# Sharing one buffer pool between activation pairs and every second weight pair in a down projection

## The chip, the cores and the metric

The kernel runs on one core of one Trainium2 chip. The metric is the device time of one execution in microseconds (us); the time of a kernel is the median of its runs. Beside the times there is one profiled execution of the kernel before, with a record of each instruction on the engines TensorE (PE), VectorE (DVE), ScalarE (ACT), GpSimd (POOL) and on the DMA-issuing queue of SyncE (SP).

## The reference, cut to what matters

The reference is one layer of a decoder trunk over 1024 tokens of 1024 channels, all in float32: a token mixer, then a feed-forward block. The change lies in the last step of the feed-forward block, the down projection:

```python
def _conv_ffn(h, ffn_up, ffn_conv_w, ffn_conv_b, ffn_down):
    hid = h @ ffn_up.astype(h.dtype)
    hid = _causal_dwconv(hid, ffn_conv_w, ffn_conv_b)
    gate, up = hid[..., :D_FF], hid[..., D_FF:]
    return (jax.nn.gelu(gate, approximate=True) * up) @ ffn_down.astype(h.dtype)
...
x = x + _rms_norm(f, norm_post_ffn[i])
```

The gated activations are 1024 x 2816 and `ffn_down` is 2816 x 1024. Behind the product come a norm over the 1024 channels and the addition of the residual.

## The kernel before, in words

**Pairs.** Each float32 operand of a matmul is split into a high part, rounded by a cast on ACT, and a low part, the rest, from a subtraction on DVE or POOL (`split`, L153 to L156). A product of two operands is three matmuls: high by high, high by low and low by high. Activations are split on ACT and DVE, streamed weights on ACT and POOL. All tiles here are 128 x 512.

**Seven products.** The down projection (`ffn_down`, L949) cuts the activations into two token halves and two halves of the 2816 rows (A11, A12, A21, A22), the weights likewise (B11 to B22), and takes seven products in place of eight, in a scheme of Strassen's kind. This text calls them P1 to P7, in the order of the code: P1 A11 by B11, P2 a difference of activations by a sum of weights, P3 A12 by B21, P4, P5 and P6 combinations, P7 the last activation combination by B22. The combined weights were summed earlier and lie in memory as `sums`. Each product goes over 11 pieces j (HT = 11). A piece is one activation pair and one weight pair, and 12 matmuls on them: 3 for each of four 128-token tiles t, each into its own PSUM bank. Four banks X take P1, P3, P5 and P7, four banks Y take P2, P4 and P6.

**Work between the products.** After piece j's activation is split, a function `then(j)` runs: in P4 `after4` (A22 gets A21 added), in P5 `after5` (A11 is replaced by A22 less A11) and in P6 `after6` (A12 is replaced by A12 less A11); each is one DVE operation on two SBUF tiles (L959). They depend on one another and on the tiles, not on the matmuls of their product. When a product is done, its four banks are taken away by `after(t)`. Behind P6 that is `second`, which finishes the second token half, behind P7 `last`; both end in `ffn_out` (L932), which loads the residual x, takes the norm's factor (DVE, then POOL) and writes the output.

**Buffers.** Activation pairs of all products share `h1p`, a pool of 16 tiles, so 8 pairs; before the down projection the same 16 tiles hold the normed activations of the up projection. Streamed weights land in `wr` (3 tiles); their pairs use `wh` and `wl`, 2 tiles each. `f2p` has 6 tiles, for s3 in P2, the junk output of squares, the raw held weights and the residual x.

**Held weights.** The last HELD = 7 weight pairs of P7 are loaded and split early, by `hold`, called from `after5` (at every third j) and `after6` (at every second j). Their pairs lie in `hp`, a pool of 16 tiles which holds A21 and the first five tiles of A22 until these have been used: the k-th held pair needs tiles 2k and 2k+1 free. Their low parts come from DVE (`split(hi, lo, raw, not held)`). P7 runs its first 4 pieces over all four banks, and then the 7 held pieces bank by bank, 21 matmuls for each, so that a bank can be taken away while the next one is worked on.

**Order.** Each engine runs its own queue in order. A planner fixes these queues when the kernel is built, from priorities and its own estimates. Splits, `then(j)` and the weights' loads are in `high_priority` blocks and go ahead of the rest as soon as their buffers are free; buffers of a pool are handed out in the order of the program.

Lines that matter: L156 `split`'s two operations, L163 the weights' load, L129 the matmuls, L959 the DVE operations in `tt`, L993 the squares in `norm`, L939 and L945 residual load and output, L944 the last DVE operation.

Of the kernel before, what the change touches and what calls it, by code (L numbers as in the profile page):

```python
# [12 lines left out]
F32 = mybir.dt.float32  # L13
F32R = mybir.dt.float32r
# [7 lines left out]
P = 128  # L22
# [16 lines left out]
HT = FT // 2  # L39
# [2 lines left out]
LN_EPS = 1e-5  # L42
GN_EPS = 64e-5

HELD = 7
DECAY = math.exp(-0.5)


# [46 lines left out]
class Trunk:  # L95
# [35 lines left out]
    def after(self, i, first):  # L131

        self.tc.add_manual_dep(
            i.ins, first.ins.name,
            mybir.DependencyInfo(mybir.DependencyClass.NoSync, mybir.DependencyReason.DATA),
            reason="the bank's first matmul clears it")
# [18 lines left out]
        eng = self.nc.gpsimd if pool else self.nc.vector  # L155
        return self.nc.scalar.copy(hi, src), eng.tensor_tensor(lo, src, hi.bitcast(F32), ALU.subtract)  # L156

    def weight(self, src, shape, home=None, held=False):

        with self.tc.high_priority():  # L160
            raw = (self.f2p.tile(shape, F32, tag="f2", name=self.nm("wr")) if held else
                   self.wp.tile(shape, F32, tag="wr", bufs=3, name=self.nm("wr")))
            self.nc.sync.dma_start(raw, src)  # L163
            if held:
                hi, lo = (self.hp.tile(shape, F32R, tag="h", name=self.nm("w")) for _ in range(2))
            elif home:
                hi, lo = (home[0].tile(shape, F32R, tag=t, bufs=BUFS[t], name=self.nm("wm")) for t in home[1:])
            else:
                hi, lo = (self.wp.tile(shape, F32R, tag=t, bufs=2, name=self.nm(t)) for t in ("wh", "wl"))
            self.low = self.split(hi, lo, raw, not held)[1]  # L170
        return hi, lo


# [773 lines left out]
    def ffn_down(self, acts):  # L947
        nc = self.nc
        first = self.tc.high_priority  # L949
        A11, A12, A21, A22 = acts[0][:HT], acts[0][HT:], acts[1][:HT], acts[1][HT:]  # L950
        B = lambda r, c: lambda j: self.a["ffn_down"][c, r * HT + j]
        T = lambda n: lambda j: self.sums[n - 1, j]
        X = [self.bank() for _ in range(4)]
        Y = [self.bank(("pb", "pn")[t // 2]) for t in range(4)]
        halves = lambda: [row[:, c * 512:(c + 1) * 512] for row in (self.row("nrow", 4) for _ in range(2)) for c in range(2)]
        four = lambda: [self.tp.tile([P, 512], F32, tag="tp", name=self.nm("c")) for _ in range(4)]

        def tt(out, a, b, op=ALU.add):
            nc.vector.tensor_tensor(out, a, b, op)  # L959
            return out  # L960

        def s3(j):
            return tt(self.f2p.tile([P, HALF], F32, tag="f2", name=self.nm("s3")), A11[j], A21[j], ALU.subtract)

        def product(banks, src, wt, start, after, then=lambda j: None, held=(), soon=True):
            ops, n = [], HT - len(held)
            for j in range(HT):
                with first():
                    hi, lo = self.pair("a", self.h1p)
                    self.split(hi, lo, src(j))  # L970
                    then(j)
                wh, wl = self.weight(wt(j), [P, 512]) if j < n else held[j - n]
                op = (hi, wh), (hi, wl), (lo, wh)
                if j >= n:
                    ops.append(op)
                else:
                    for t in range(4):
                        mms(banks[t], t, op, start and j == 0, j == HT - 1)

            ins = []  # L980
            for t in range(4):
                for i, op in enumerate(ops):
                    ins += mms(banks[t], t, op, False, i == len(held) - 1)
                with first() if soon else ExitStack():
                    after(t)
            self.chain(ins)

        def mms(ps, t, op, start, stop):
            return [self.mm(ps, a[:, t * P:(t + 1) * P], w, start=start and i == 0, stop=stop and i == 2, skip=True)
                    for i, (a, w) in enumerate(op)]  # L990

        def norm(h, t, c, f, src, junk):
            nc.scalar.activation(junk, src, AF.Square, accum_out=self.fss[:, 4 * h + t, c:c + 1])  # L993
            tt(f, src, self.post_ffn[:, c * 512:(c + 1) * 512], ALU.mult)

        s1, s7 = halves(), halves()
        product(X, lambda j: A11[j], B(0, 0), True, lambda t: nc.scalar.copy(s1[t], X[t]))
        product(Y, s3, T(3), True, lambda t: nc.scalar.copy(s7[t], Y[t]))
        c11 = four()
        product(X, lambda j: A12[j], B(1, 0), False, lambda t: norm(  # L1000
            0, t, 0, c11[t], X[t], self.f2p.tile([P, 512], F32, tag="f2", name=self.nm("junk"))))
        c21 = four()
        late = []

        def hold(j, every=2):

            if j % every == 1 and len(late) < HELD:
                late.append(self.weight(B(1, 1)(HT - HELD + len(late)), [P, 512], held=True))


        def after4(j):
            tt(A22[j], A21[j], A22[j])

        def after5(j):
            hold(j, 3)
            tt(A11[j], A22[j], A11[j], ALU.subtract)

        def after6(j):
            hold(j)
            tt(A12[j], A12[j], A11[j], ALU.subtract)  # L1020

        product(Y, lambda j: A22[j], T(4), False, lambda t: tt(c21[t], s1[t], Y[t]), after4)
        product(X, lambda j: A22[j], T(1), True, lambda t: tt(s7[t], s7[t], X[t]), after5)

        def second(t):
            tt(c21[t], c21[t], Y[t])
            tt(s1[t], s1[t], Y[t])
            norm(1, t, 0, c21[t], c21[t], Y[t])
            tt(s7[t], s7[t], s1[t])
            norm(1, t, 1, s7[t], s7[t], Y[t])  # L1030
            self.ffn_out(4 + t, (c21[t], s7[t]))

        def last(t):
            tt(s1[t], s1[t], X[t])
            norm(0, t, 1, s1[t], s1[t], X[t])
            self.ffn_out(t, (c11[t], s1[t]))

        product(Y, lambda j: A11[j], T(2), True, second, after6, soon=False)
        product(X, lambda j: A12[j], B(1, 1), False, last, held=late)
# [258 lines left out]
```

## Time and profile before

| | |
|---|---|
| median of 3 runs | 1340.19 us (1337.7 to 1342.9) |
| the profiled execution | 1338.02 us, of which the span is 1336.2 us |
| mean granted TensorE clock in it | 0.982 |
| PE busy | 1266.3 us of the span, 95% |
| DVE busy | 860.7 us, 64% |
| ACT busy | 679.6 us, 51% |
| POOL busy | 618.8 us, 46% |

Times in the trace count from the start of the span. The down projection runs from about 1089 us to the end. PE is the busiest engine by far, so what matters is where it is not busy, and why. "Idle before" with a releaser in a row of the trace is the time for which the engine had nothing running, and who ended it.

### The profile page before, as it was taken

The page shows a single profiled execution, that of the slowest core. Times are in us where ns is not written, and L with a number is a line of the kernel's source. Part 1 is how long each engine was busy: PE and PEld are TensorE (multiplying, and loading weights), DVE is VectorE, ACT ScalarE, POOL GpSimd, SP SyncE. Part 2 cuts the span into 40 slices and gives each one's busy share as a digit, 9 for nine tenths or more (in the row PEclk, how much of TensorE's full clock was granted, in tenths as well). Part 3 has the DMA queues.
Part 4 walks back from the last instruction along what each step waited for, and adds up shares of the span by engine and source line. Part 5 has one row for each costly group of instructions (what it writes and reads, how often), then busy time and mean ns, then how long its engine had stood idle before and what let it go on. Part 6 is the DMA issues. An engine that isn't in the chain of part 4 may idle for free. (4 is left out here: it accounts for less than half of the span.)

```text
span 1336.2 us, 22956 instructions
## 1 busy us (share of the span) xinstructions
PE 1266.3 (95%) x8580; PEld 1019.7 (76%) x8580; DVE 860.7 (64%) x1450; ACT 679.6 (51%) x1354; POOL 618.8 (46%) x522
## 2 busy tenths in 40 slices
PE   6999989999899989999999999999999989996996
PEld 5767767777678767787798788888888878875885
DVE  5377998997799989885521463455555365295347
ACT  6563654657755765656543564333333344443451
POOL 4343423354333322444462467667676454445441
PEclk9999979999999999999999999999999999997998
DMA  6322211222123441222355655665654323343325
GB/s 213 79 77 62 72 40 49 52 69 56 50 66 104 149 144 50 64 72 79 103 162 172 234 197 179 199 191 178 197 177 139 95 79 95 95 122 123 95 80 204
DMA packets 85647, 155.79 MB, mean 117 GB/s; under 512 B 9280, under 2 KB 15808, under 8 KB 85536
## 3 DMA queue, kind: packets, MB, share of 16 engines
q1 hardware_dynamic: 85536, 154.33, 38.1%
q8 instruction: 67, 1.10, 0.4%
q14 instruction: 44, 0.36, 0.1%
HBM read 129.13 MB, written 25.17 MB: 115 GB/s over the span
## 5 line engine op out<-in xcount | busy, mean ns | idle before, releaser
L156 POOL TENSOR_TENSOR wl<-wr,wh 128x512 fp32r<-128x512 f32 x350 | 474.9, 1358 | 548.9 <-ACT wh L156 522.2
L129 PE MATMUL pb<-f,wh 128*128 128x512 f32 x1408 | 442.3, 395 | 3.2 <-ACT pb L771 1.8
L156 ACT CAST wh<-wr 128x512 fp32r<-128x512 f32 x350 | 215.1, 615 | 326.5 <-PE pb L129 167.4
L129 PEld LDWEIGHTS pb<-f,wh 128*128 128x128 f32 x1408 | 263.7, 188 | 61.9 <-ACT pb L771 2.0
L129 PE MATMUL pb<-f,wl 128*128 128x512 f32 x704 | 280.1, 398 | 2.0 <-POOL wl L156 2.0
L129 PE MATMUL pb<-h,wh 128*128 128x512 f32 (+3 forms) x720 | 229.8, 399 | 2.5 <-ACT wh L156 1.9
L877 DVE SCALAR_TENSOR_TENSOR acc<-pb,params,acc 128x511 f32<-128x511 f32 (+1 forms) x128 | 95.5, 746 | 183.8 <-ACT acc L872 123.9
L399 DVE SCALAR_TENSOR_TENSOR pc<-c,params,pc 128x512 f32<-128x512 f32 x232 | 174.2, 751 | 4.6 <-ACT pc L396 0.5
L129 PEld LDWEIGHTS pb<-f,wl 128*128 128x128 f32 x704 | 132.6, 188 | 35.7 <-POOL wl L156 5.4
L129 PEld LDWEIGHTS pb<-h,wh 128*128 128x128 f32 (+2 forms) x720 | 132.3, 189 | 34.4 <-ACT wh L156 4.3
L129 PE MATMUL pb<-h,wl 128*128 128x512 f32 (+3 forms) x360 | 146.7, 408 | 3.0 <-POOL wl L156 2.8
L129 PE MATMUL pb<-wh,a 128*128 128x512 f32 x428 | 141.9, 400 | 3.4 <-ACT wh L156 3.4
L129 PEld LDWEIGHTS pb<-wh,a 128*128 128x128 f32 x428 | 81.4, 191 | 23.8 <-ACT wh L156 4.3
L129 PE MATMUL pb<-wl,a 128*128 128x512 f32 x214 | 86.7, 405 | 11.3 <-POOL wl L156 11.3
L129 PEld LDWEIGHTS pb<-h,wl 128*128 128x128 f32 (+2 forms) x360 | 68.1, 189 | 22.3 <-POOL wl L156 5.8
L156 DVE TENSOR_TENSOR a<-act,a 128x512 fp32r<-128x512 f32 x50 | 37.3, 746 | 66.1 <-ACT a L156 66.1
L156 ACT CAST a<-act 128x512 fp32r<-128x512 f32 x50 | 31.0, 621 | 71.7 <-PE pn L129 47.5
L129 PEld LDWEIGHTS pb<-wl,a 128*128 128x128 f32 x214 | 41.1, 192 | 23.1 <-POOL wl L156 13.3
L877 DVE SCALAR_TENSOR_TENSOR pt<-pb,params,pt 128x511 f32<-128x511 f32 (+1 forms) x48 | 35.8, 746 | 33.7 <-ACT ecarry L874 33.1
L917 POOL TENSOR_TENSOR b<-b,b 128x512 f32<-128x512 f32 x44 | 57.0, 1295 | 0.9
L872 ACT ACTIVATE acc<-pb,params 128x512 f32<-128x512 f32 x64 | 49.5, 774 | 1.8 <-PE pb L129 1.8
L129 PE MATMUL pn<-wh,a 128*128 128x512 f32 x132 | 47.8, 403 | 0.0
(297 smaller groups left out, 1928.3 us busy)
## 6 DMA issues: line engine op xcount, KB each, us to landing
wr<-ffn_up SPq DMA_DIRECT2D x176, 256.0 KB, 2.7
wr<-w_in SPq DMA_DIRECT2D x80, 256.0 KB, 2.6
b<-ffn_down SPq DMA_DIRECT2D x44, 256.0 KB, 4.0
sums<-b SPq DMA_DIRECT2D x44, 256.0 KB, 2.4
wr<-sums SPq DMA_DIRECT2D x44, 256.0 KB, 2.6
wr<-ffn_down SPq DMA_DIRECT2D x33, 256.0 KB, 2.6
wr<-w_out SPq DMA_DIRECT2D x32, 256.0 KB, 2.7
mixd<-t SPq DMA_DIRECT2D x16, 256.0 KB, 3.2
```

The lines of the kernel that those rows point to most:

```text
L129: return self.nc.tensor.matmul(out, lhsT, rhs, start=start, stop=stop, skip_group_check=skip)
L156: return self.nc.scalar.copy(hi, src), eng.tensor_tensor(lo, src, hi.bitcast(F32), ALU.subtract)
L399: nc.vector.scalar_tensor_tensor(out, c[:, j:j + HALF], w(j), acc, ALU.mult, ALU.add)
L872: nc.scalar.activation(acc, ps, AF.Identity, scale=w(2), bias=self.par("fb", ch))
L877: nc.vector.scalar_tensor_tensor(acc[:, o:], ps[:, :HALF - o], w(j), acc[:, o:], ALU.mult, ALU.add)
L917: sub = lambda o, x, y, op=ALU.subtract: nc.gpsimd.tensor_tensor(o, x, y, op)
```

## The change

Weight pairs of odd pieces (j = 1, 3, 5, ...) of all seven products no longer take `wh`/`wl` but a pair from `h1p`, the activations' 16 tiles; even pieces keep `wh`/`wl` to themselves. HELD goes from 7 to 5, so P7 streams 6 pieces and holds 5. The low part of a held weight is now made on POOL, like that of any other weight. The raw tile of an odd piece still comes from `wr`; only that of a held weight comes from `f2p`.

```diff
-HELD = 7
+HELD = 5
...
-    def weight(self, src, shape, home=None, held=False):
+    def weight(self, src, shape, home=None, held=None):
 
         with self.tc.high_priority():
-            raw = (self.f2p.tile(shape, F32, tag="f2", name=self.nm("wr")) if held else
+            raw = (self.f2p.tile(shape, F32, tag="f2", name=self.nm("wr")) if held is self.hp else
                    self.wp.tile(shape, F32, tag="wr", bufs=3, name=self.nm("wr")))
             self.nc.sync.dma_start(raw, src)
             if held:
-                hi, lo = (self.hp.tile(shape, F32R, tag="h", name=self.nm("w")) for _ in range(2))
+                hi, lo = self.pair("w", held)
             elif home:
...
-            self.low = self.split(hi, lo, raw, not held)[1]
+            self.low = self.split(hi, lo, raw, True)[1]
...
-                wh, wl = self.weight(wt(j), [P, 512]) if j < n else held[j - n]
+                wh, wl = self.weight(wt(j), [P, 512], held=self.h1p if j % 2 else None) if j < n else held[j - n]
...
-                late.append(self.weight(B(1, 1)(HT - HELD + len(late)), [P, 512], held=True))
+                late.append(self.weight(B(1, 1)(HT - HELD + len(late)), [P, 512], held=self.hp))
```

`pair` takes two 128 x 512 tiles from the pool it is given.

## The prediction

> **What bounds the kernel now.** I read the page first: PE is busy for 95% of the span, so only its gaps count. The table by stage, one row for a product, shows where they are.
>
> ```profile
> span 1336.2 us, 22956 instructions
> ```
>
> ```profile
> core 0: us, PE busy (x) PEld busy (x) DVE busy (x) ACT busy (x) POOL busy (x), PEclk, DMA share, GB/s
> ...
> 1186.80:1232.50 45.70, 34.44 (x132) 25.93 (x131) 32.08 (x47) 17.29 (x35) 22.44 (x11) 0.85 0.43 138
> 1232.50:1263.30 30.80, 30.80 (x133) 24.80 (x133) 11.15 (x17) 12.56 (x22) 14.21 (x12) 1.00 0.35 94
> ...
> 1294.40:1325.60 31.20, 31.18 (x134) 24.79 (x132) 27.45 (x52) 11.16 (x29) 7.89 (x9) 1.00 0.42 136
> ```
>
> P5, the middle row, runs at PE's pace: 133 matmuls in 30.80 us; so does P7 below it. P4, the first row, takes 45.70 us for 132. At P5's pace these are 30.6 us, so P4 loses 15.1 us. The timeline of PE shows how, and a second, smaller loss at the start of P1.
>
> ```profile
> 1089.33 1.09 PE L129 MATMUL pb<-wh,a 128*128 128x512 f32 x4
> 1093.92 0.80 PE L129 MATMUL pb<-wl,a 128*128 128x512 f32 x1 [3.50 <-POOL wl L156]
> ...
> 1097.07 1.32 PE L129 MATMUL pb<-wh,a 128*128 128x512 f32 x5
> ```
>
> ```profile
> 1205.62 0.74 PE L129 MATMUL pb<-wh,a 128*128 128x512 f32 x2 [3.04 <-ACT wh L156]
> ...
> 1214.68 0.79 PE L129 MATMUL pb<-wl,a 128*128 128x512 f32 x1 [7.49 <-POOL wl L156]
> ...
> 1219.95 0.40 PE L129 MATMUL pb<-wl,a 128*128 128x512 f32 x1
> ```
>
> Both times PE waits for the low part of a weight. In P4, at j = 5, it first waits 3.04 us for the high part, then 7.49 us for the low one, and after so long an idle time the next 12 matmuls, from 1214.68 to 1219.95, take 5.27 us in place of 2.8 (the granted clock is 0.85 in P4's row): 2.5 us more. At the start of P1 it is 3.50 us idle, and 7 matmuls from 1093.92 to 1097.07 that take 3.15 us in place of 1.6: 5.0 us in all. Next, why POOL and ACT were late.
>
> ```profile
> 1168.48 1.29 POOL L156 TENSOR_TENSOR wl<-wr,wh 128x512 fp32r<-128x512 f32 x1 [1.51 <-ACT wh L156]
> ...
> 1205.64 10.21 POOL L156 TENSOR_TENSOR wl<-wr,wh 128x512 fp32r<-128x512 f32 x2 [5.93 <-ACT wh L156]
> ```
>
> ```profile
> 1203.91 0.62 ACT L156 CAST w<-wr 128x512 fp32r<-128x512 f32 x1 [5.98 <-DVE act L959]
> ```
>
> ```profile
> 1168.64 1.68 DVE L959 TENSOR_TENSOR act<-act,act 128x512 f32<-128x512 f32 x1
> ...
> 1206.20 0.68 DVE L156 TENSOR_TENSOR a<-act,a 128x512 fp32r<-128x512 f32 x1
> 1206.80 1.28 DVE L959 TENSOR_TENSOR act<-act,act 128x512 f32<-128x512 f32 x2
> 1208.01 0.69 DVE L156 TENSOR_TENSOR a<-act,a 128x512 fp32r<-128x512 f32 x1
> ...
> 1212.22 1.29 DVE L959 TENSOR_TENSOR act<-act,act 128x512 f32<-128x512 f32 x2
> ```
>
> A split on POOL costs 1.29 us. A DVE operation on two SBUF tiles comes every 0.60 us when they follow one another (1206.20, 1206.80, and 1208.01 after two more). The two engines exclude each other: the DVE operation at 1168.64 takes 1.68 us because POOL had begun at 1168.48 and ended at 1169.77. The other way round it is worse: from 1206.20 to 1213.5 DVE never pauses, and the POOL split begun at 1205.64 comes through only behind that run (two splits take 10.21 us where they cost 2.6). ACT was late for the same reason: its queue stood 5.98 us in front of a held weight's cast, which waited for `after4` on DVE to free a tile of `hp`, with P4's own cast behind it.
>
> The Trainium skill ("SBUF — State Buffer", section "Who interferes with whom") has the exclusion: a DVE instruction with two SBUF inputs contends with a GpSimd instruction that reads SBUF, and whichever issues first holds the pair for its whole instruction. The 1.68 us row agrees. By that text POOL's turn would come after one DVE instruction; here the row at 1205.64 shows it waiting through a dozen. If POOL did get its turn each time, the sum below would end at its lowest loss, 5.2 us in P4.
>
> How full is that common resource? The groups of DVE and POOL from 1167.26 to 1214.64:
>
> ```profile
> L959 DVE TENSOR_TENSOR act<-act,act 128x512 f32<-128x512 f32 x17 | 14.6, 871 | 0.1
> L156 DVE TENSOR_TENSOR a<-act,a 128x512 fp32r<-128x512 f32 x13 | 10.0, 768 | 2.1 <-ACT a L156 2.1
> L959 DVE TENSOR_TENSOR row<-act,row 128x512 f32<-128x512 f32 x8 | 9.5, 1186 | 0.2
> L959 DVE TENSOR_TENSOR act<-act,row 128x512 f32<-128x512 f32 x8 | 7.4, 920 | 0.0
> L156 DVE TENSOR_TENSOR w<-wr,w 128x512 fp32r<-128x512 f32 x6 | 4.5, 766 | 0.0
> L959 DVE TENSOR_TENSOR c<-pb,post_ffn 128x512 f32<-128x512 f32 x4 | 2.6, 677 | 0.0
> ```
>
> ```profile
> L156 POOL TENSOR_TENSOR wl<-wr,wh 128x512 fp32r<-128x512 f32 x13 | 26.1, 2013 | 22.8 <-ACT wh L156 22.8
> ```
>
> 52 DVE operations with two SBUF inputs (17 + 13 + 8 + 8 + 6) at 0.60 us are 31.2 us; 12 whole POOL splits (the 13th only begins there) at 1.29 us are 15.5 us. Together 46.7 us of 47.4: the pair is full for the whole stretch. Its load is the 33 operations of `after4` to `after6`, which run here all at once though P6 and P7 need most of them much later. So the bound in P4 is this common port, and the weights, only two ahead, pay first.
>
> **The change, part by part.**
>
> *More lead for weights, less for activations.* A weight pair is needed 2.80 us after the one before it:
>
> ```profile
> 1239.81 1.29 POOL L156 TENSOR_TENSOR wl<-wr,wh 128x512 fp32r<-128x512 f32 x1 [1.51 <-ACT wh L156]
> 1242.61 1.29 POOL L156 TENSOR_TENSOR wl<-wr,wh 128x512 fp32r<-128x512 f32 x1 [1.51 <-ACT wh L156]
> ```
>
> Now the pair for j + 2 is free when j is done: 2.80 us of lead. Afterwards even pieces wait for j - 4, so 8.4 us, or 5.6 us where pieces 10 and 0 meet; odd pieces share 8 pairs in which two pieces take three, a lead of 11.2 us. Activations fall from 19.6 us (8 pairs ahead) to 11.2 or 14. This by itself adds no instruction; DMA loads keep their three raw tiles in front.
>
> *The crowded stretch moves.* P4's first activation pair was the ninth from P3's first and came free after piece 3:
>
> ```profile
> 1167.26 0.62 ACT L156 CAST a<-act 128x512 fp32r<-128x512 f32 x1 [1.66 <-PE pb L129]
> ```
>
> In the new order (a0 a1 w1 a2 a3 w3 a4 a5 w5 ...) the ninth pair is w5, two pieces later: 1167.3 + 5.6 = 1172.9. From there I add what must be through before P4's last piece can run, at the same prices. DVE: 11 splits and 33 operations of `after4` to `after6`, 44 x 0.60 = 26.4 us. POOL: the last weight of P3 and the 11 of P4, 12 x 1.29 = 15.5 us.
>
> *Held weights.* Their low parts leave DVE (6 in the stretch, 3.6 us, counted out above) and go to POOL: four of the five come ahead of P4's last weight, 4 x 1.29 = 5.2 us. For the shared port this is a loss of 1.6 us, and in POOL's queue P4's and P5's weights stand behind them.
>
> Sum: 26.4 + 15.5 + 5.2 = 47.1 us, so the last piece's operands are there at 1220.0. Unhindered, PE starts piece 10 at 1186.8 + 28.0 = 1214.8. P4 then loses 5.2 us where the turns fall well. It loses 7.6 if the four `c` operations (2.4 us, one input from PSUM) don't fit beside POOL, and up to 10.1 if the idle time comes in one piece and brings the 2.5 us of slow matmuls again. I take 7, near the middle: the old stretch had 46.7 of 47.4 us filled without the `c` operations, so most of these do fit beside POOL, but DVE's unbroken runs remain. Gain in P4: 15.1 - 7 = 8.1 us. After P4 the port has room (P5's row: DVE 11.15 and POOL 14.21 of 30.80), so nothing new is late there.
>
> *Start of P1.* The unbroken DVE run there is these operations:
>
> ```profile
> L156 DVE TENSOR_TENSOR a<-row,a 128x512 fp32r<-128x512 f32 x7 | 4.5, 684 | 0.0
> L959 DVE TENSOR_TENSOR s<-row,act 128x512 f32<-128x512 f32 x4 | 2.5, 686 | 0.0
> ```
>
> Two of the first eight pairs now go to w1 and w3, so up to two splits (1.2 us) leave the run; w0 keeps its two buffers, and w1's split may stand before it in POOL's queue (1.29 us). Bounds: 1.3 us lost to 5.0 us gained; I take 1 us gained, two splits fewer being the certain part.
>
> *The end.* With five held pairs a bank's last group is 15 matmuls, not 21. The chain of work that ended last does not go through them:
>
> ```profile
> 1293.42 0.69 DVE c L959
> ...
> 1310.33 0.07 DVE ss L941
> ...
> 1314.37 3.46 DMA out<-x
> ...
> 1317.85 4.19 DMA x<-x1d
> ...
> 1323.10 5.12 DMA out<-x
> ```
>
> It goes from P6's end over `second` on DVE and then over the reuse of `f2p` tiles, output by output. Banks of P7 finish 4.2, 2.8, 1.4 and 0 us later than before, which this chain hides: row 0's second residual lands only at 1322.0, and P7's first bank would be done at 1294.4 + 6 x 2.8 + 3.5 = 1314.7. But two more activation splits fall into `second` (6 in place of 4, since P7's pairs are shared as well): 2 x 0.60 = 1.2 us on the chain. Bounds: nothing, and the rival below.
>
> Total against the profiled execution's own 1338.0 us (1.8 us of it around the span): -8.1 - 1.0 + 1.2 = -7.9, so 1330.1. The median of the runs shown is 2.2 us above that execution, so I forecast 1332.3 us. With P4's loss from 5.2 to 10.1 us and the start and end within a microsecond or so, this case alone spans 1328 to 1337. About 0.5%, 6.7 us, is what a measurement of this kernel can tell from no change.
>
> **The rivals.**
>
> *The stall goes altogether.* If the planner queues `after5` and `after6` later, since activations come later, the port is no longer full, and weights 8.4 us ahead bridge a 7.3 us DVE run. Then 15.1 and up to 5.0 us come back, less 1.2: 1340.2 - 18.9 = 1321.3. Against it: those operations keep their priority and depend on `after4` alone.
>
> *The stall only moves.* DVE runs through without a pause to the tenth piece (10 x 2.4 + 2.4 us), POOL having done 9 splits (11.6 us): 1172.9 + 38.0 = 1210.9. Then two held splits stand before w6 in POOL's queue: 3 x 1.29, 1214.8. Pieces 6 to 10 follow, 14.0 us and 2.5 us of slow clock: P4 ends at 1231.3, where 1217.6 is ideal, 13.7 us lost. Gain 1.4 + 1.0 - 1.2 = 1.2, so 1339.0. For it: the run from 1206.20 on, and ACT's 5.98 us before a held cast, which the change keeps, for four or five held pairs still wait for `after4`. Against it: 7.3 us of run are less than the 8.4 us of new lead.
>
> *Slower: P7's streamed weights starve.* P7 now streams w4 and w5 too. In `second` DVE worked without a pause up to 1310.3:
>
> ```profile
> L959 DVE TENSOR_TENSOR nrow<-nrow,nrow 128x512 f32<-128x512 f32 x4 | 3.8, 958 | 0.0
> L959 DVE TENSOR_TENSOR c<-c,post_ffn 128x512 f32<-128x512 f32 x4 | 3.7, 954 | 0.0
> L156 DVE TENSOR_TENSOR a<-act,a 128x512 fp32r<-128x512 f32 x4 | 2.7, 681 | 0.0
> ```
>
> If POOL gets no turn there, w4's low part is ready at 1310.3 + 1.3 = 1311.6. PE needs it at 1294.4 + 11.2 + 0.9 = 1306.5 (four matmuls into piece 4), so 5.1 us are lost, w5 adds 1.3 and the slow clock 2.5: 8.9 us. It decides from a run of DVE that lasts past 1305.2. With a stall in P4 that only moves: 1339.0 + 8.9 = 1347.9. Against it: the first two rows hold operations stretched to 0.95 us on average, so POOL did get turns there.
>
> **How the numbers follow.** The forecast case 0.54, gone altogether 0.12, only moved 0.21, slower 0.13. Faster by over 0.5% means below 1333.5: about three quarters of the forecast case (0.40) and the first rival (0.12), 0.52. Slower by over 0.5% means above 1346.9: most of the last, 0.11. The rest is 0.37. The range reaches to the first rival's time, 1321, and over the second into the third, 1343.
>
> **What would show it.** P4's window should be some 37 us long with PE waits of a few microseconds in the pieces from j = 6 on, not 10.5 us at j = 5; P4's first cast at about 1172 rather than 1167; five more POOL splits and no `w` on DVE; DVE still without a pause for some microseconds; the start of P1 nearly as before; the time from P6's end to the end of the span about 43 us (1336.2 - 1294.4 = 41.8 before, and 1.2). I am wrong if P4 has no wait left, if its wait is again over 10 us, or if PE waits inside P7.

## The result and the profile after

| | before | after |
|---|---|---|
| median of the runs | 1340.19 us (1337.7 to 1342.9) | 1325.42 us (1324.58 to 1327.54) |
| profiled execution, its span | 1338.02, 1336.2 us | 1325.43, 1323.6 us |
| mean granted TensorE clock in it | 0.982 | 0.984 |

The ratio of the times is 0.9892, with a 95% interval from 0.9874 to 0.9909: 14.8 us gained between the medians, where 7.9 were forecast. The page's head, and the table by stage for P1, P4, P5, P7 and the time behind PE's last matmul (columns: window, its length, busy time and count of each engine, granted clock, DMA share, GB/s):

```profile
span 1323.6 us, 22932 instructions
```

```profile
core 0: us, PE busy (x) PEld busy (x) DVE busy (x) ACT busy (x) POOL busy (x), PEclk, DMA share, GB/s
1091.80:1122.70 30.90, 30.90 (x135) 24.98 (x134) 29.80 (x30) 16.09 (x29) 18.23 (x13) 1.00 0.39 111
1184.00:1219.30 35.30, 32.97 (x133) 25.75 (x132) 35.20 (x36) 14.61 (x29) 24.95 (x15) 0.95 0.50 159
1219.30:1250.10 30.80, 30.80 (x134) 24.91 (x133) 19.67 (x24) 13.44 (x25) 16.53 (x12) 1.00 0.35 101
1280.40:1311.30 30.90, 30.90 (x133) 24.60 (x131) 27.28 (x52) 11.54 (x30) 9.52 (x9) 1.00 0.40 131
1311.30:1323.60 12.30, 0.00 (x1) 0.00 (x0) 6.22 (x13) 1.08 (x4) 1.10 (x2) 0.64 0.74 247
```

P1 runs at PE's pace from its first matmul, P4 lasts 35.3 us, P7 has no gap. From the first matmul of a product to that of the next (to the last matmul's end for P7), the two traces give:

| us | P1 | P4 | P5 | P7's start to the end | P1's start to the end |
|---|---|---|---|---|---|
| before | 36.0 | 46.1 | 30.8 | 41.6 | 246.9 |
| after | 30.7 | 35.3 | 30.7 | 43.2 | 231.9 |

So P1 gave 5.3 us, P4 10.8, and the end took 1.6 back. P2, P3, P5 and P6 take 30.8 us each before and 30.7 after, 0.5 us in all. (P1 begins 2.4 us later in the profile after, behind work that the change does not touch; 2.0 us of this are there by 516 us. This is why the two spans differ by 12.6 us and the stretch from P1 to the end by 15.0.) The waits of PE from 1080 us to the end, first before, then after (releaser, us in total, times, longest):

```profile
PE pb L129 <- POOL wl L156: 11.3, 4, 7.5
PE pb L129 <- ACT wh L156: 3.4, 2, 3.0
```

```profile
PE pb L129 <- DVE a L156: 1.4, 2, 0.7
PE pb L129 <- POOL wl L156: 0.9, 1, 0.9
```

The long waits for weights are gone. What is left in P4, in the timeline of PE after, comes late and is short:

```profile
1207.40 0.50 PE L129 MATMUL pb<-wl,a 128*128 128x512 f32 x1 [0.94 <-POOL wl L156]
1208.55 0.84 PE L129 MATMUL pb<-wh,a 128*128 128x512 f32 x2 [0.65 <-DVE a L156]
...
1216.65 0.73 PE L129 MATMUL pb<-wh,a 128*128 128x512 f32 x2 [0.75 <-DVE a L156]
```

P4's last piece would have begun at 1184.0 + 28.0 = 1212.0. Its activation releases PE at 1216.65, 4.6 us late: 2.3 us in these three waits, the rest in slower matmuls behind them (PE was busy for 32.97 us with what takes 30.8). DVE, busy for 35.20 of 35.30 us, is the bound there: the port is still full, as the forecast said. How the two engines share it is seen in their timelines after, POOL first:

```profile
1194.82 3.32 POOL L156 TENSOR_TENSOR w<-wr,w 128x512 fp32r<-128x512 f32 x2 [0.68 <-DMA wr<-sums]
1198.11 1.74 POOL L156 TENSOR_TENSOR wl<-wr,wh 128x512 fp32r<-128x512 f32 x1
```

```profile
1195.21 1.78 DVE L959 TENSOR_TENSOR row<-act,row 128x512 f32<-128x512 f32 x1
1196.91 1.78 DVE L156 TENSOR_TENSOR a<-act,a 128x512 fp32r<-128x512 f32 x1
1198.61 1.78 DVE L959 TENSOR_TENSOR act<-act,row 128x512 f32<-128x512 f32 x1
```

In this stretch they alternate strictly, one DVE operation and one POOL split every 1.70 us; DVE's records of 1.78 us hold its wait for POOL. With 0.60 us for DVE's part, POOL's is 1.10 us and not the 1.29 us that a split lasts alone.

### The profile page after: what moved, and what is told of

It is laid out like the page before. It is cut to its first block, busy times and chain, and to the rows that moved or that the text cites. A ratio compares the mean times of both kernels' runs of the same rounds, so it can differ in the third digit from the quotient of the medians.

```text
span 1323.6 us, 22932 instructions
## 1 busy us (share of the span) xinstructions
PE 1261.0 (95%) x8580; PEld 1015.9 (77%) x8580; DVE 875.1 (66%) x1443; ACT 679.7 (51%) x1354; POOL 624.8 (47%) x529
## 5 line engine op out<-in xcount | busy, mean ns | idle before, releaser
L156 POOL TENSOR_TENSOR wl<-wr,wh 128x512 fp32r<-128x512 f32 (+1 forms) x319 | 425.4, 1335 | 481.7 <-ACT wh L156 448.6
L156 ACT CAST wh<-wr 128x512 fp32r<-128x512 f32 (+1 forms) x319 | 195.9, 615 | 317.9 <-PE pb L129 162.1
L129 PE MATMUL pb<-w,a 128*128 128x512 f32 x366 | 89.8, 393 | 0.0
L129 PE MATMUL pb<-wh,a 128*128 128x512 f32 x240 | 82.1, 398 | 1.4 <-DVE a L156 1.4
L129 PEld LDWEIGHTS pb<-w,a 128*128 128x128 f32 x366 | 68.8, 188 | 16.2
L156 POOL TENSOR_TENSOR w<-wr,w 128x512 fp32r<-128x512 f32 x38 | 54.1, 1429 | 49.1 <-ACT w L156 46.1
L156 DVE TENSOR_TENSOR a<-act,a 128x512 fp32r<-128x512 f32 x50 | 46.2, 947 | 38.7 <-ACT a L156 38.7
L156 ACT CAST w<-wr 128x512 fp32r<-128x512 f32 x38 | 23.5, 620 | 64.1 <-PE pn L129 16.0
L129 PEld LDWEIGHTS pb<-wh,a 128*128 128x128 f32 x240 | 45.1, 189 | 12.8 <-DVE a L156 2.1
```

Of the source, the lines that this page charges most:

```text
L129: return self.nc.tensor.matmul(out, lhsT, rhs, start=start, stop=stop, skip_group_check=skip)
```

## The experiments

The theory at the start was the forecast's: the longer lead of the weights lets PE outlast DVE's runs (the expectations call it A). Against it stood that it is the five held pairs with their low parts on POOL (C), the shorter lead of the activations (B), which moves the crowd of `after4` to `after6`, or the crowd itself. Of DVE's runs that POOL has to wait through, a later theory (D) said that they come from POOL and DVE starting within 0.05 us of each other; its rival was that POOL keeps its turn as long as its queue is fed. All results in one table (lengths read as above; "long split" is the longest POOL split in P4's stretch over 2.3 us):

| kernel | median us | ratio to before, 95% | P1 | P4 | P7's start to end | long split |
|---|---|---|---|---|---|---|
| after | 1325.42 | 0.9892 (0.9874 to 0.9909) | 30.7 | 35.3 | 43.2 | none |
| e1_share_only | 1329.52 | 0.9929 (0.9907 to 0.9951) | 30.7 | 42.0 | 40.9 | 11.47 |
| e2_held_only | 1339.94 | 0.9998 (0.9986 to 1.001) | 36.1 | 42.4 | 45.5 | none |
| e3_own4 | 1329.4 | 0.9926 (0.9908 to 0.9944) | 30.7 | 41.4 | 41.1 | 8.98 |
| e4_short_lead | 1334.66 | 0.9956 (0.994 to 0.9972) | 31.6 | 44.3 | 41.4 | 6.58 |
| e5_share_h5_dve | 1332.45 | 0.9933 (0.9913 to 0.9953) | 30.7 | 41.9 | 43.2 | 10.87 |
| e6_share_h7_pool | 1330.11 | 0.9922 (0.9904 to 0.9939) | 30.7 | 40.3 | 41.0 | none |
| e7_shift | 1339.12 | 0.9994 (0.9979 to 1.0009) | 36.1 | 44.3 | 42.2 | 8.11 |
| e8_after_late | 1320.16 | 0.9849 (0.9834 to 0.9863) | 30.7 | 31.6 | 43.8 | none |
| e9_h7_late | 1322.92 | 0.9862 (0.9839 to 0.9885) | 30.7 | 31.3 | 40.9 | none |
| e10_before_late | 1324.61 | 0.989 (0.9865 to 0.9916) | 36.1 | 32.1 | 42.3 | none |
| e11_after_shift | 1330.61 | 0.9946 (0.9914 to 0.9977) | 31.4 | 37.8 | 43.6 | none |

**e1_share_only** has the sharing alone; HELD stays 7 and held low parts stay on DVE. Against the kernel after:

```diff
-HELD = 5
+HELD = 7
...
-            self.low = self.split(hi, lo, raw, True)[1]
+            self.low = self.split(hi, lo, raw, held is not self.hp)[1]
```

> The change without its second half: odd weight pairs share the activations' 16 tiles, but seven pairs are held again and their low parts come from DVE again. Theory A (the weights' longer lead, 8.4 to 11.2 us in place of 2.8, bridges what POOL loses to DVE): P4 35 to 38 us (46.1 before, 35.3 with the whole change), P1 31 us (35.9 before), ratio to before 0.988 to 0.993. Theory C (fewer held pairs, and six DVE operations fewer in the crowded stretch, are what helps): P4 44 us or more, ratio 0.998 to 1.003.

P1 has its whole gain, P4 only 4.1 of 10.8 us, so its 42.0 us lie between what A and C forecast. POOL's timeline in P4:

```profile
1201.01 11.47 POOL L156 TENSOR_TENSOR w<-wr,w 128x512 fp32r<-128x512 f32 x1 [5.86 <-PE pn L129]
```

A split of 1.29 us waits through DVE's run, longer than before. The lead doesn't prevent this, and doesn't cover it: PE waits 9.8 us for it.

**e2_held_only** is the other half: five held pairs, low parts on POOL, no sharing. Against the kernel before (lines that only rename the argument `held` are left out):

```diff
-HELD = 7
+HELD = 5
...
-            self.low = self.split(hi, lo, raw, not held)[1]
+            self.low = self.split(hi, lo, raw, True)[1]
```

> The other half alone: five held pairs with low parts from POOL, all streamed weights in wh/wl as before. Theory A: weights are two ahead as before, so P4 stays at 43 to 48 us and P1 at 36 us; ratio 0.997 to 1.003. Theory C: P4 35 to 38 us, ratio 0.990 to 0.993.

P4 gains 3.7 us without a long split, P1 nothing, and the end loses 3.9 (P7 itself takes 32.0 us, with a PE wait of 0.5 us for a streamed `wl` two ahead): nothing in the sum. Neither half is the change; 4.1 + 3.7 is less than 10.8.

**e3_own4** gives the odd weights four tiles of their own, and the activations keep their 8 pairs. It takes the lead out of the change and nothing else. Against the kernel before:

```diff
-    def weight(self, src, shape, home=None, held=False):
+    def weight(self, src, shape, home=None, held=False, odd=None):
...
+            elif odd:
+                hi, lo = self.pair("w", odd)
...
+        self.vp = pool("vp", 4)
...
-                wh, wl = self.weight(wt(j), [P, 512]) if j < n else held[j - n]
+                wh, wl = self.weight(wt(j), [P, 512], odd=self.vp if j % 2 else None) if j < n else held[j - n]
```

> The kernel before, but odd weight pairs get four tiles of their own: weights are about four ahead, activations stay eight pairs ahead, seven pairs are held and their low parts come from DVE. Theory A: P4 33 to 37 us and P1 31 us; from P1's first matmul to the end 229 to 235 us (246.9 before, 231.8 with the change). Theory B (the gain comes from the activations' shorter lead, which puts the crowd of DVE operations later and spreads it): P4 44 us or more, P1 36 us.

P1 gains its 5.3 us, P4 4.7. POOL's timeline and the waits of PE in e3:

```profile
1203.05 8.98 POOL L156 TENSOR_TENSOR w<-wr,w 128x512 fp32r<-128x512 f32 x1 [8.34 <-PE pn L129]
```

```profile
PE pb L129 <- POOL w L156: 8.6, 1, 8.6
```

One wait is left in the whole down projection, nearly as long as the split's. So the odd weights' own tiles explain P1 alone, and P4 only in part.

**e4_short_lead** takes three of the activations' 8 pairs away, from P1's piece 5 to the end of P5, and leaves the weights alone. Against the kernel before:

```diff
+        hog = []
...
+                if j == 5 and not hog:
+                    for _ in range(3):
+                        hog.extend(self.pair("hog", self.h1p))
+                    for x in hog:
+                        nc.vector.memset(x[:, 0:1].bitcast(F32), 0.0)
...
-        product(X, lambda j: A22[j], T(1), True, lambda t: tt(s7[t], s7[t], X[t]), after5)
+        def free(t):
+            tt(s7[t], s7[t], X[t])
+            if t == 0:
+                for x in hog:
+                    x = x[:, 0:1].bitcast(F32)
+                    tt(x, x, s7[0][:, 0:1])
+
+        product(X, lambda j: A22[j], T(1), True, free, after5)
```

> The kernel before, but three of the eight pairs of the activations' pool are taken out from P1's sixth piece until P5 is done (one-column operations on six tiles at either end, nothing else): activations are five ahead, weights two ahead. Theory A: no gain in P4, 43 to 48 us, ratio 0.998 to 1.004. Theory B: P4 35 to 40 us, ratio 0.990 to 0.995.

P4 gains 1.8 us: the shorter lead of the activations is a small part at most. Unlooked for, P1 lost 4.4 of its 5.3 us of delay: the planner put the memsets into DVE's run at the start of P1, and there POOL's wait ended (3.65 us in place of 6.64).

**e5_share_h5_dve** is the kernel after with held low parts on DVE again; **e6_share_h7_pool** is it with seven held pairs:

```diff
-            self.low = self.split(hi, lo, raw, True)[1]
+            self.low = self.split(hi, lo, raw, held is not self.hp)[1]
```

```diff
-HELD = 5
+HELD = 7
```

> The change with the held weights' low parts back on DVE; five are held and odd pairs are shared as in the change. Sharing alone left one POOL operation waiting 11.5 us in P4 (P4 42.0 us), the whole change none (P4 35.3 us). If it is the low parts on POOL that make the difference: P4 40 to 43 us, a POOL wait over 5 us, ratio to before 0.993. If it is the number of held pairs: P4 35 to 37 us, ratio 0.989 to 0.990.

> The change with seven held pairs, their low parts on POOL. If the low parts on POOL keep POOL in turn with DVE: P4 35 to 37 us with no POOL operation over 2.3 us; with seven held pairs the time from P7's start to the end goes back from 43.2 to 41 us, so a ratio of 0.987 to 0.989. If the number of held pairs counts: P4 40 to 43 us, ratio 0.993.

With DVE (e5) the long split is there, 10.87 us, and P4 takes 41.9. On POOL with seven pairs (e6) no split is long, and yet P4 takes 40.3 us. ACT's and PE's timelines in e6 show why:

```profile
1212.39 0.62 ACT L156 CAST w<-wr 128x512 fp32r<-128x512 f32 x1 [5.38 <-DVE act L959]
...
1217.69 0.62 ACT L156 CAST w<-wr 128x512 fp32r<-128x512 f32 x1 [3.64 <-DVE a L156]
...
1218.74 0.61 ACT L156 CAST wh<-wr 128x512 fp32r<-128x512 f32 x1
```

```profile
1219.40 0.50 PE L129 MATMUL pb<-wh,a 128*128 128x512 f32 x1 [1.32 <-ACT wh L156]
1221.85 0.62 PE L129 MATMUL pb<-wl,a 128*128 128x512 f32 x1 [1.94 <-POOL wl L156]
```

ACT's queue stands at the casts of the last held pairs until DVE frees their tiles, and the streamed weight's cast of 1218.74 stands behind them. HELD = 5 takes two such casts out of the crowd, 5.0 us in P4 (40.3 to 35.3), and costs 2.2 us at the end (41.0 to 43.2; e5 against e1 says 2.3).

**e7_shift** moves POOL's start against DVE's: a cast of one column on ACT follows each weight's cast in the down projection, so that the split is released later. Against the kernel before; **e11_after_shift** is the same edit in the kernel after:

```diff
-        self.n = 0
+        self.n, self.down = 0, False
...
-        return self.nc.scalar.copy(hi, src), eng.tensor_tensor(lo, src, hi.bitcast(F32), ALU.subtract)
+        return (self.nc.scalar.copy(hi, src), pool and self.down and self.nc.scalar.copy(hi[:, 0:1], src[:, 0:1]), eng.tensor_tensor(lo, src, hi.bitcast(F32), ALU.subtract))[::2]
...
-        first = self.tc.high_priority
+        first, self.down = self.tc.high_priority, True
```

> The kernel before; in the down projection a one-column cast on ACT follows each weight's cast, so that POOL's split of it begins a little later against DVE's operations; weights stay two ahead. In the six profiles so far all POOL splits of over 3 us begin within 0.05 us of the start of a DVE operation in an unbroken run, and nearly all others get the port behind the DVE operation that is running. Theory D (such a collision makes the long waits, lead or not): the two long waits of 6.6 and 9.0 us go, unless a new one is hit; P1 31 to 33 us, P4 36 to 41 us, ratio 0.992 to 0.996. Theory A (lead is what it takes): P1 35 us or more, P4 43 us or more, ratio 0.998 to 1.005.

> The changed kernel with a one-column cast on ACT behind each weight's cast in the down projection, so that POOL's splits begin at other moments against DVE's operations. If it was by luck of these moments that the changed kernel has no long POOL wait: one of over 5 us appears, P4 38 to 42 us, ratio 0.993 to 0.997. If a POOL queue that is kept fed takes its turns whatever the moment: none, P4 35 to 37 us, ratio 0.989 to 0.992.

The moments moved and the waits stayed. In e7, P4's long split (two splits in the row) starts 0.32 us behind the start of a DVE operation and still waits:

```profile
1203.69 9.34 POOL L156 TENSOR_TENSOR wl<-wr,wh 128x512 fp32r<-128x512 f32 x2 [5.00 <-ACT wh L156]
```

e11 shows no long split, as the fed queue says, but that alone is no proof of it: P4 is 2.5 us longer than in the kernel after, P1 and P5 0.7 each, the runs are wide (1328.81 to 1338.86 us), and the ratio, 0.9946, is the one forecast for a long wait. The trace of the kernel after speaks against the fed queue. There a split begins after 3.10 us without POOL work, in the middle of six DVE operations that follow one another, and has its turn at once (POOL's row, then DVE's):

```profile
1210.44 1.60 POOL L156 TENSOR_TENSOR w<-wr,w 128x512 fp32r<-128x512 f32 x1 [3.10 <-ACT w L156]
```

```profile
1209.02 5.88 DVE L959 TENSOR_TENSOR act<-act,act 128x512 f32<-128x512 f32 x6
```

**e8_after_late** spreads the crowd: each operation of `after4` to `after6` is queued on DVE behind the activation split of its own piece, and no earlier. Against the kernel after; **e10_before_late** is the same edit in the kernel before, and **e9_h7_late** is e8 with HELD = 7:

```diff
-                    self.split(hi, lo, src(j))
-                    then(j)
+                    with self.tc.issue_after(self.split(hi, lo, src(j))[1].ins):
+                        then(j)
```

> The changed kernel, with each of the operations after4 to after6 queued on DVE behind its own piece's activation split, so that they run in P4, P5 and P6 and not all at once in P4. If the crowd on the port is what is left of P4's loss: P4 30.8 to 32 us, P5 and P6 still 30.7 us, from P1's first matmul to the end 227 to 229 us (231.9 with the change), ratio to before 0.984 to 0.987. If P4's rest has another cause (casts in ACT's queue behind held weights, loads): P4 34 us or more.

> The kernel before, with after4 to after6 spread over their own products and nothing else: weights two ahead, seven held, low parts on DVE. If the crowd of DVE operations is the cause of P4's loss, and the change only bridges it: P4 31 to 33 us, P1 36 us as before, from P1's first matmul to the end 231 to 233 us, ratio 0.988 to 0.991. If weights need more lead in any case: P4 38 us or more, ratio 0.994 or more.

> The changed kernel with after4 to after6 spread over their own products (as in e8), and seven held pairs in place of five. If the casts of the sixth and seventh held pair, which wait for tiles of A22, block ACT's queue as they did in e6: P4 34 us or more, ratio 0.986 to 0.989. If spreading the operations frees these tiles in time: P4 31 to 32 us, and from P7's start to the end 41 us in place of 43.8, so from P1's first matmul to the end 226 to 227 us and a ratio of 0.982 to 0.985, the fastest of all.

P4's row in the table by stage, e8 and then e10:

```profile
1182.80:1214.40 31.60, 31.17 (x134) 24.65 (x133) 28.33 (x25) 14.82 (x29) 23.80 (x15) 1.00 0.58 179
```

```profile
1185.20:1217.30 32.10, 31.49 (x133) 24.51 (x132) 28.91 (x29) 15.16 (x31) 15.21 (x11) 1.00 0.52 156
```

DVE has room again, PE hardly waits. This one edit in the kernel before brings P4 from 46.1 to 32.1 us with weights two ahead and held low parts on DVE, and about the same time as the whole change (0.989). In P4, then, the crowd is the cause, together with the held weights, which are begun inside `then(j)` and moved with it: before, all seven held casts on ACT and all seven low parts on DVE lie in P4, in e10 three and two. Of PE's waits in P4 before, 7.8 us ended with POOL and 3.4 us with ACT; e10 takes both away and does not tell the port from ACT's queue. On top of the change the edit gives the fastest kernel of this study, 1320.16 us, with the interval wholly below that of the kernel after. e9 is shorter from P1 to the end in its profile (227.6 against 228.7 us), but its median is not better, and the intervals overlap: HELD of 5 or 7 is not told apart there. It misses its forecast of 0.982 to 0.985, and P5 takes 32.7 us in it, with one PE wait of 1.75 us for a low part from POOL.

**e12_port** measures the port by itself: 96 times a run of 14 DVE operations with two SBUF inputs, and one POOL subtraction released by an ACT cast whose width grows by 8 columns each time, so that the release walks through DVE's 0.60 us.

```python
for o in outs:
    nc.vector.tensor_tensor(o, g, y, ALU.subtract)
nc.gpsimd.tensor_tensor(p, z, t1[:, :512] if w <= 512 else t1[:, w - 512:w], ALU.subtract)
```

> Measures the port alone; the whole computation is left out and the output is filler. In 96 trials a run of 14 DVE subtractions of two SBUF tiles (128x512, 0.60 us apart) meets one POOL subtraction that ACT releases, in each trial some 7 ns later than in the one before. If the moment decides: splits that begin within 0.05 us of a DVE operation's start last to the end of the run (over 4 us), all others 1.3 to 1.9 us. If POOL always gets its turn: none over 1.9 us. If DVE keeps the port through any unbroken run: nearly all over 4 us.

Its groups and one trial in the timeline of POOL:

```profile
L116 DVE TENSOR_TENSOR o<-g,y 128x512 f32<-128x512 f32 x1344 | 920.2, 757 | 3.3
L117 POOL TENSOR_TENSOR p<-z,t 128x512 f32<-128x512 f32 x96 | 143.1, 1491 | 855.7 <-ACT t L113 570.9 <-ACT t L114 284.8
```

```profile
101.39 1.48 POOL L117 TENSOR_TENSOR p<-z,t 128x512 f32<-128x512 f32 x1 [8.94 <-ACT t L113]
```

The mean is 1.49 us; the 96 lie between 1.26 and 1.82 us and fall evenly with the time since DVE's last start (1.80 at 0.006 us, 1.62 at 0.183, 1.26 at 0.589, then 1.82 again). In every trial POOL had its turn behind the DVE operation then running, also in the seven that began within 0.05 us after a DVE start and the eight within 0.05 us before one. Release moments from 0.09 to 0.18 us behind a DVE start did not occur. Starting together is thus not enough for a long wait, and by e7 not needed: theory D falls. That POOL waits through a whole run needs something that this loop does not have.

## Why the prediction came out as it did, point by point

**The time: in the range, for a gain of nearly twice the forecast.** 1325.42 us lies below the 1328 to 1337 us of the forecast case alone and nearer to the first rival's 1321.3 than to 1332.3. The gain from P1 on was 15.0 us where 7.9 were forecast: 2.7 us more in P4, 4.3 more at the start of P1, 0.4 less at the end and 0.5 in the products between.

**The bound: right.** The crowd is what bounds P4 (e10), and the change leaves the common port full (DVE busy for 35.20 of 35.30 us). The loss before was 15.3 us rather than 15.1, since the window of the forecast ends 0.5 us before P5's first matmul. The crowd's start moved as worked out: P4's first activation cast is the second of this pair, at 1170.3, 13.7 us before P4 begins; 1172.9 stood 13.9 before it.

```profile
1169.80 1.14 ACT L156 CAST a<-act 128x512 fp32r<-128x512 f32 x2 [1.63 <-PE pb L129]
```

**P4: the sum right, one price too high.** Forecast were 5.2 to 10.1 us lost, 7 taken, 8.1 gained; measured 4.6 and 10.8. The term at fault is 1.29 us for each of 16 POOL splits. At the 1.10 us that a turn takes, 26.4 + 17.6 = 44.0 us; from DVE's first operation of the crowd this ends at 1215.8, and PE's last wait ended at 1216.65. (The trace has 41 such DVE operations and 18 whole splits up to there, 44.4 us by the same prices, so two errors in the counts nearly cancel.) That the sum came out is in part luck: it takes for granted that POOL has its turns, and what gave it these was not the lead, as the paragraph on the argument from lead shows.

```profile
1171.84 0.69 DVE L959 TENSOR_TENSOR act<-act,act 128x512 f32<-128x512 f32 x1
```

**The start of P1: the step that failed.** "I take 1 us gained, two splits fewer being the certain part", bounds 1.3 lost to 5.0 gained: it was 5.3. The size was reckoned from the splits that leave DVE's run, and not from POOL's wait for that run, which went away whole. e3 shows that the odd weights' own tiles are enough: there no activation split leaves the run, and P1 gains the same. It is not that w0 comes earlier: its cast begins 2.80 us before P1's first matmul in both traces (1086.53 and 1088.97). The timelines show what is different. Before, POOL and the run of DVE begin together at 1087.23, and POOL comes through only with the first DVE operation that is not of this kind, at 1092.66:

```profile
1092.06 0.69 DVE L156 TENSOR_TENSOR a<-row,a 128x512 fp32r<-128x512 f32 x1
1092.66 0.75 DVE L877 SCALAR_TENSOR_TENSOR acc<-pb,params,acc 128x511 f32<-128x511 f32 x1
```

After, POOL has w1's split first, goes straight on to w0's and takes turns with DVE; PE has the low part before it asks for it:

```profile
1089.09 1.29 POOL L156 TENSOR_TENSOR w<-wr,w 128x512 fp32r<-128x512 f32 x1 [0.92 <-ACT w L156]
1090.33 1.82 POOL L156 TENSOR_TENSOR wl<-wr,wh 128x512 fp32r<-128x512 f32 x1
```

So w1's split ahead of w0's, put down as a price of up to 1.29 us, was no loss. Why POOL has its turn there and had to wait before is part of what stays open below.

**The argument from lead: half right.** "7.3 us of run are less than the 8.4 us of new lead" did not hold: with the lead alone (e1, e3) PE waited 9.8 and 8.6 us. In P4 the long split goes where held low parts are on POOL (after, e2, e6, e9, e11, e8) or the crowd is spread (e10), and stays in all six kernels with them on DVE and the crowd in one piece. The forecast counted this move as a loss of 1.6 us on the port; taking e5 against the kernel after, it is a gain of 6.6 us in P4. The runs show that the move does it, and not by which mechanism.

**Held weights on ACT: cheaper than feared.** ACT still stands 6.16 and 5.39 us before held casts after the change, but with five pairs instead of seven P4's last cast no longer waits behind them (e6).

**The end: size near, place wrong.** Forecast 1.2 us lost by two more splits in `second`, measured 1.6. The chain of work that ended last after the change does not bear out the place:

```profile
1295.48 0.07 DVE var L150
...
1310.55 5.51 DMA out<-x
...
1316.45 2.60 DMA out<-x
```

Its part on DVE ends 15.1 us after P7's start (1295.48 against 1280.4), before it was 16.0 (1310.4 against 1294.4). The loss goes with HELD = 5 in three pairs of kernels (2.2, 2.3 and 2.9 us), and with seven pairs the sharing loses nothing there (40.9 and 41.0 against 41.6). All of it lies behind PE's last matmul: 10.7 us before (1325.6 to 1336.2), 12.3 after. The later banks, put at nothing, cost it, probably in the transfers at the end; that part is only argued.

**The rivals.** The stall did not go altogether (4.6 us stayed in P4) nor only move. e8 does by hand what the first rival expected of the planner, and comes to 1320.16 us where that rival said 1321.3. P7's weights did not starve with the lead; without it (e2) P7 took 32.0 us.

**What stays open:** why POOL takes its turn at once in one run of DVE and waits through another. From 1080 us on, the traces of eight kernels have 11 POOL splits of 3.65 to 11.47 us, and each wait ends with DVE's run: behind its last operation, or at the first that is a memset or reads PSUM. Ten of the eleven began within 0.05 us of a DVE start, the eleventh did not; but in the thirteen kernels some forty others that began so in a run of DVE had their turn at once (1.29 to 1.84 us). None of the eleven began straight behind another POOL split. Runs of DVE operations that each wait on a semaphore, as in the kernel, were not tried by themselves.

## What to carry to other kernels

Where two engines share a port, look first at what fills it and when it has to be done: work that a priority releases early crowded out the splits that PE needed next, and putting it in step with its own pieces was worth as much as all the new buffers. More buffers must be tested alone: for the odd weights they took away the wait at the start of P1, while in P4 a wait stayed, longer in e1 than before. An engine's queue is also a place in line: two casts that could not start yet held up the one that PE needed (e6).

## What the runs showed of the hardware

A POOL subtraction that lasts 1.29 us alone takes 1.10 us of the port when POOL and DVE alternate, worked out from a pitch of 1.70 us and 0.60 us for DVE. The Trainium skill ("SBUF — State Buffer", section "Who interferes with whom") says that the pair is held for a whole instruction; e12 agrees in all 96 trials (1.26 to 1.82 us), while the eleven long waits, up to 11.47 us, are more than that rule gives. The same section says that a DVE instruction with at most one SBUF input, outside the modes that use two ports, doesn't contend with GpSimd; the wait before P1 that ended with the operation reading `pb` at 1092.66 agrees.
